# Half of the attention's interleaving copies on ScalarE beside VectorE's, rows of 256 columns in other places and orders, a smaller DMA scratch, six chains moved

## The chip, the cores and the metric

The kernel runs on one core of a Trainium2 chip. Times are device microseconds of one execution, read as the median of several. One execution each is also recorded by the hardware profiler; all views below are of that recorded execution, and its times count from its first instruction. The engines are PE (TensorE: matmuls; PEld is its loading of weights), DVE (VectorE), ACT (ScalarE), POOL (GpSimd) and SP (SyncE, which here only issues DMAs).

## What is computed

Two decoder layers over 256 rows of width 1024, in float32. Cut to what matters:

```python
for i in range(2):
    proj = rms_norm(x, norm_g[i]) @ w_in[i]                  # 1024 x 4096
    rq, rk, rv, rz, mq, mk, mv, mz = split(proj, 8)          # 512 columns = 4 heads of 128 each
    r_out = silu(rz) * group_norm(retention(rotary(rq), rotary(rk), rv)) * ret_norm_g[i]
    m_out = silu(mz) * attention(rms_norm(mq), rms_norm(mk), mv, rel_bias)   # causal, 256 rows
    x = x + concat(r_out, m_out) @ w_out[i]                  # 1024 x 1024
    gate = sigmoid(rms_norm(x) @ w_ple_gate[i])              # 1024 x 1024
    x = x + gate * rms_norm(p[i] @ w_ple[i]) * ple_norm_g[i]
```

With 256 rows there is one block of keys, so the attention is plain causal attention (`moba`), and the retention has two chunks of 128 rows.

## The kernel before, in words

**Precision by three products.** A float32 operand is cut into a high part (rounded to the type fp32r) and a low part (the rest). A product is three matmuls: high by high, high by low, low by high (`mm3`, L386 to L388; `first_rows`, L534, for the first input tiles; `three`, L913, for the scores of attention and retention). The stationary operand is 128x128 of the activations, the moving one a row of 512 weight columns, so most matmuls are 128x512. Three places have rows of 256 columns: the scores (L913: 256 keys, four calls of 12 matmuls), the first four matmuls on the first tile, and the last tile of the last gate projection, which is done in two halves of 256 columns (`gated`, `mm3` with `cols`: 48 matmuls).

**Weights.** Tiles of 128 x 2 x 512 floats (512 KB) are loaded by SP into the ring `wst` (8 buffers), cut on ACT (L336, high part `wh`) and on DVE (L339, low part `wl`) into rings of 5, or into lent space of T, V, PS, K2 and G when the attention doesn't use it. Each weight tile feeds 12 matmuls. The host lays columns of weights in lanes: a row of 512 is read as four runs of 32 pieces of 16 bytes (`columns`, `lanes`).

**Turning activations round.** Results have rows of the sequence on the partitions; the next product needs them the other way. `halves` (L602, ACT) takes a 128x512 float32 tile apart into two planes of 16 bits, `turned` (L607) has SP transpose both planes by one DMA (L612), and two copies on DVE (L621, one for each plane, 128x512 of 16 bits) interleave them again in the target. `to_heads` does that for the queries and keys of both attentions (target T, 8 calls a layer), `probs` for the probabilities (target PS, 3 calls a layer), `to_parts` for the inputs of the next projection (target tmp).

**Order.** All five engines run instructions in the order in which the program is recorded. PE's order is nearly fixed by the code. For the other engines a planner, `Flow`, keeps a clock for each engine, adds an assumed cost for each step and, among the steps that could start, takes the one of the chain with the smallest due time (`key`). `tick` puts the attention's matmul groups between rows of a projection once the chains that they need are done by the planner's clocks. So an assumed cost, a due time or one more buffer moves instructions on ACT, DVE, POOL and SP.

**Around the places that matter.** In layer 0 the order on PE is: first tiles (L534), projections (L386 to L388) with the attention's scores (L931, L913) between them, the attention's sums over values and retention's own scores (L941, L991), retention's scores (L913) and sums (L941), then the output projection. `ret_norm` (L1008 to L1029) and `ret_gate` (L1050 to L1066) follow the retention's sums; the tile that L1057 reads is one of four PSUM banks `acc` that the output projection needs next.

## Time and profile before

| | |
|---|---|
| median of 3 runs | 298.32 us (297.07 to 298.73) |
| the profiled execution | 296.44 us, its span from first to last instruction 294.5 us |
| granted TensorE clock | 1.000 over the span |
| DVE busy | 253.8 us (86%), 461 instructions |
| ACT busy | 214.5 us (73%), 376 instructions |
| POOL busy | 33.1 us (11%) |
| DMA | 69.77 MB, mean 237 GB/s; queue q1 (issued by SP) 78.7% of 16 engines, q0 (issued by POOL) 32 packets |
| last matmul starts | 290.18 us; the tail behind it is one tanh, two VectorE operations and a store |

A matmul's listed duration overlaps the next one, since they are pipelined: what it costs is the distance between starts. An idle time in brackets at the end of a row of the timeline is that of the engine just before it, with what ended it.

### The profile page before, as it was taken

Reading aid. Unit: us, or ns where it says so; the run is one execution under the profiler, and the core shown is the slowest. Engines: PE = TensorE matmul, PEld = TensorE weight load, DVE = VectorE, ACT = ScalarE, POOL = GpSimd, SP = SyncE. Lnnn points to the kernel's source line nnn. Section 1 sums busy time; section 2 is a strip of 40 time slices with the busy share of each in tenths; the row PEclk is TensorE's granted clock in tenths of the full one; section 3 lists DMA queues with packets and bytes.
Section 4 is the critical chain, followed back from the end, with each engine's and each line's share of the span. In section 5 each row is a group of like instructions: output and inputs, shape, how many; then the busy total and the mean of one; then the engine's idle time right before and its main releaser. Section 6 shows DMA issues by size and latency. Waiting matters only on the chain.

```text
span 294.5 us, 4301 instructions
## 1 busy us (share of the span) xinstructions
PE 289.2 (98%) x1411; PEld 247.2 (84%) x1411; DVE 253.8 (86%) x461; ACT 214.5 (73%) x376; POOL 33.1 (11%) x44
## 2 busy tenths in 40 slices
PE   8999999999999999999999999999999999999994
PEld 5888888888899878888888888888898988888894
DVE  4958699979999999699999589999998797969942
ACT  4889965789837893998585896599646869489411
POOL 5005200000001200022003240000000030001200
PEclk9999999999999999999999999999999999999999
DMA  7999989988989958698679969687999776843011
GB/s 233 368 402 416 260 251 330 364 270 164 232 249 248 358 140 280 157 240 329 157 228 258 376 197 254 247 226 168 241 330 238 269 229 181 277 95 71 0 75 71
DMA packets 61774, 69.77 MB, mean 237 GB/s; under 512 B 46260, under 2 KB 47160, under 8 KB 61624
## 3 DMA queue, kind: packets, MB, share of 16 engines
q1 hardware_dynamic: 61712, 69.50, 78.7%
q8 instruction: 11, 0.18, 0.2%
q14 instruction: 11, 0.09, 0.1%
q0 software_dynamic: 32, 0.01, 0.0%
q10 hardware_dynamic: 8, 0.00, 0.0%
HBM read 57.42 MB, written 1.05 MB: 199 GB/s over the span
## 4 chain that ended last, share of the span: by engine, by line
PE 73%; DVE 13%; DMA 5%; ACT 4%; issue 3%; ACTq 0%; DVEq 0%
PE acc L386 20%; PE acc L387 19%; PE acc L388 19%; DVE wl L339 5%; PE acc L534 5%; DMA wst<-in_w_ple 3%; DMA w<-u 2%; PE mix L941 2%; ACT wh L336 2%; DVE T L621 2%; PE mix L282 1%; PE mix L723 1%; PE mix L724 1%; PE mix L725 1%; PE mix L913 1%
## 5 line engine op out<-in xcount | busy, mean ns | idle before, releaser
L386 PE MATMUL acc<-wh,a 128*128 128x512 f32 (+1 forms) x286 | 108.1, 378 | 0.0
L387 PE MATMUL acc<-wl,a 128*128 128x512 f32 (+1 forms) x286 | 107.6, 376 | 0.0
L388 PE MATMUL acc<-wh,a 128*128 128x512 f32 (+1 forms) x286 | 107.5, 376 | 0.0
L339 DVE TENSOR_TENSOR wl<-wst,wh 128x1024 fp32r<-128x1024 f32 x76 | 92.1, 1221 | 7.2 <-ACT wh L336 6.7
L336 ACT CAST wh<-wst 128x1024 fp32r<-128x1024 f32 x76 | 78.5, 1052 | 13.4 <-PE acc L388 4.0
L388 PEld LDWEIGHTS acc<-wh,a 128*128 128x128 f32 x286 | 53.5, 187 | 9.2
L386 PEld LDWEIGHTS acc<-wh,a 128*128 128x128 f32 x286 | 53.5, 187 | 8.9
L387 PEld LDWEIGHTS acc<-wl,a 128*128 128x128 f32 x286 | 53.5, 187 | 8.6
L602 ACT COPY u<-tok 128x1024 uint16<-128x1024 uint16 x30 | 30.9, 1048 | 13.9 <-DVE tok L959 8.9
L638 ACT CAST a<-tmp 128x512 fp32r<-128x512 f32 x20 | 12.4, 618 | 11.0 <-DVE tmp L635 8.3
L654 POOL TENSOR_TENSOR ro<-rs_t,neghalf 128x4 f32<-128x4 f32 x4 | 5.8, 1460 | 127.6 <-DVE rs_t L652 127.6
L602 ACT COPY u<-x_t 128x1024 uint16<-128x1024 uint16 x12 | 12.5, 1042 | 9.8 <-DVE x_t L1119 6.8
L621 DVE COPY tmp<-w 128x512 uint16<-128x512 uint16 x40 | 16.3, 463 | 0.1
L1163 ACT ACTIVATE tmp<-acc,hr 128x512 f32<-128x512 f32 (+1 forms) x9 | 5.7, 638 | 13.4 <-PE acc L388 13.4
L621 DVE COPY T<-w 128x512 uint16<-128x512 uint16 x32 | 12.9, 468 | 2.6 <-DMA w<-u 2.6
L640 DVE TENSOR_TENSOR a<-tmp,a 128x512 fp32r<-128x512 f32 x20 | 13.7, 684 | 0.0
L814 POOL TENSOR_TENSOR qr<-qms,neghalf 128x4 f32<-128x4 f32 x8 | 10.5, 1317 | 11.8 <-DVE qms L812 11.8
L1166 DVE SCALAR_TENSOR_TENSOR tmp<-tmp,E 128x512 f32<-128x512 f32 (+1 forms) x9 | 5.7, 628 | 7.1 <-ACT tmp L1163 7.0
L386 PE MATMUL acc<-T,a 128*128 128x512 f32 (+1 forms) x30 | 11.1, 372 | 0.4 <-DVE tok L1057 0.4
L941 PEld LDWEIGHTS mix<-V,PS 128*128 128x128 f32 x96 | 11.3, 192 | 0.3
L941 PE MATMUL mix<-V,PS 128*128 128x128 f32 x96 | 11.4, 275 | 0.0
L534 PE MATMUL acc<-wh,a 128*128 128x512 f32 (+1 forms) x42 | 11.2, 387 | 0.0
(143 smaller groups left out, 460.9 us busy)
## 6 DMA issues: line engine op xcount, KB each, us to landing
wst<-in_w_in SPq DMA_DIRECT2D x59, 512.0 KB, 6.5
wst<-in_w_out SPq DMA_DIRECT2D x16, 512.0 KB, 7.2
wst<-in_w_gate SPq DMA_DIRECT2D x16, 512.0 KB, 4.6
wst<-in_w_ple SPq DMA_DIRECT2D x4, 512.0 KB, 7.3
wst<-in_early SPq DMA_DIRECT2D x4, 384.0 KB, 6.7
a<-in_early SPq DMA_DIRECT2D x3, 384.0 KB, 5.2
x_t<-in_x SPq DMA_DIRECT2D x1, 1024.0 KB, 11.5
gb<-in_ple_g SPq DMA_DIRECT2D x2, 512.0 KB, 7.0
```

The costliest lines, as they stand in the source:

```text
L336: nc.scalar.copy(hi, s)
L339: nc.vector.tensor_tensor(lo, s, hi.bitcast(F32), op=ALU.subtract)
L386: nc.tensor.matmul(ps, ah, wh, start=start, stop=False)
L387: nc.tensor.matmul(ps, ah, wl, start=False, stop=False)
L388: nc.tensor.matmul(ps, al, wh, start=False, stop=stop)
L534: nc.tensor.matmul(ps[m][:, sl], (a0.lo if which[0] == "lo" else a0.hi)[:, k, m * P:(m + 1) * P], columns(w, sl), start=start and i + j == ...
L602: nc.scalar.copy(u, src.bitcast(U16).rearrange("p (n t) -> p t n", t=2))
L621: nc.vector.tensor_copy(v, w[:, t].rearrange("p (h b) k -> p h (b k)", h=v.shape[1]))
L638: nc.scalar.copy(h, src)
L640: nc.vector.tensor_tensor(a.lo[:, k0:k0 + 4, m * P:(m + 1) * P], src, h.bitcast(F32), op=ALU.subtract)
L814: nc.gpsimd.tensor_tensor(r, t, neghalf[:, :H], op=ALU.pow)
L941: nc.tensor.matmul(ps[:, h * DH:(h + 1) * DH], lhs(h, m, b), v[:, b, h * DH:(h + 1) * DH], start=b == 0, stop=b == m)
```

## The change

Six edits.

1. `turned` takes `beside`. Where it is set (`BESIDE`: for `to_heads` and `probs`, not for `to_parts`), the copy of the second plane is a chain of its own, `other`, on ACT, and runs next to DVE's copy of the first plane; what follows waits for both. That is 22 of the 84 copies.
2. Rows of 256 columns: the tile Q2 (stationary operand of L913) moves from the pool `big` to the pool `cs`, and two gap tiles of 48 floats surround that place, so that it starts 64 bytes past a multiple of 128 bytes in each partition, where it started at a multiple before; K2 (moving) still starts at a multiple. The last gate weights are laid in lanes over groups of 256 columns, and `line_half` reads a half as four runs of 16 pieces, where `columns` read two runs of 32. The 512-wide row of that tile comes out in another column order, which its tanh puts right by its access pattern.
3. `dynamic_dma_scratch_size=4096`, where the default takes 16384 bytes of each partition, and one more buffer of `wst` (9).
4. `LIFT` adds numbers to the due times of six named chains; so the second query tile's norm comes earlier, and a weight load, the copies of two planes, the statistics of the second half of x and a load of layer 1 come later.
5. In `first_rows` the second tile's three products run in the order of the first tile's (low activations before low weights), and its low activations are made before its low weights.
6. The planner's assumed cost of a row of 256 columns: 0.342 for three where it was 0.36, and 0.5 of a row of 512 where it was 0.53.

```diff
-S_BUFS, H_BUFS = 8, 5
+S_BUFS, H_BUFS = 9, 5
+LIFT = {("qk_norm", 1): -5.0, ("gen", 3): 2.0, ("other", 5): 1.0, ("other", 4): 4.0, ("gen", 61): 4.0,
+        ("x_stats", 1): 4.0}
+BESIDE = True, True, False
...
+    def due(self):
+        return (self.key() if callable(self.key) else self.key) + LIFT.get(self.name, 0.0)
...
-    cs.tile([P, 32], F32, name="gap")
+    cs.tile([P, 48], F32, name="gap")
+    ct.tile([P, 48], F32, name="gap")
...
+    def line_half(w, c0):
+        return bass.AP(tensor=w.tensor, offset=w.offset + c0 + (LANES - 1) * LINE,
+                       ap=[w.ap[0], [-LINE, LANES], [LANES * LINE, S // LANES // LINE], [1, LINE]])
...
-        wh, wl = columns(wh, cols), columns(wl, cols)
+        wh, wl = (lanes(w) if cols.stop - cols.start == GW else line_half(w, cols.start) for w in (wh, wl))
...
-        firsts[k, "a"] = flow.begin(first_input(k, src, g), k - (19.6 if k else 19.9), flow.end)
+        firsts[k, "a"] = flow.begin(first_input(k, src, g), k - (19.6 if k > 1 else 19.9), flow.end)
...
-        order = [(("hi", "hi"), wh, None)] + (rows if k == 0 or key else rows[::-1])
+        order = [(("hi", "hi"), wh, None)] + (rows if k < 2 or key else rows[::-1])
...
-    def turned(u, raw, take=()):
+    def turned(u, raw, take=(), beside=False):
...
+        def other():
+            yield ask(ACT, 0.53)
+            copy(nc.scalar.copy, 1)
+            flow.free("w16")
+        if beside:
+            c = flow.begin(other(), Chain.running.key, flow.end - 0.35)
+            copy(nc.vector.tensor_copy, 0)
+            return (c,)
+        copy(nc.vector.tensor_copy, 0)
+        yield ask(DVE, 0.35)
+        copy(nc.vector.tensor_copy, 1)
...
-                both = big.tile([P, 2, H, P], F32R, name="Q2", bufs=1)
-                hi, lo = Q2[name] = both[:, 0], both[:, 1]
+                pair = cs.tile([P, 2, H, P], F32R, name="Q2")
+                hi, lo = Q2[name] = pair[:, 0], pair[:, 1]
...
-            nc.scalar.activation(th, ps, AF.Tanh, scale=HR[m, "v"])
+            if last and n and width == GW:
+                nc.scalar.activation(th.rearrange("p (s t n) -> p s t n", s=2, t=LANES),
+                                     ps.rearrange("p (t s n) -> p s t n", s=2, t=LANES), AF.Tanh, scale=HR[m, "v"])
+            else:
+                nc.scalar.activation(th, ps, AF.Tanh, scale=HR[m, "v"])
...
+    w_gate[DEPTH - 1, 1] = rows(a["w_ple_gate"][DEPTH - 1:], GW, 2, P // LINE // 2)[0, 1]
...
-    nc = bacc.Bacc("TRN2", target_bir_lowering=False, num_devices=1)
+    nc = bacc.Bacc("TRN2", target_bir_lowering=False, num_devices=1, dynamic_dma_scratch_size=4096)
```

PE keeps its instructions and, but for the second first tile and the attention's scores of layer 1 (two rows earlier among the projections), their order.

What moves on the others is shown at three places. Rows are engine order; line numbers are those of the kernel that the rows are from, so L336, L602, L612, L621, L849 before are L353, L624, L634, L642, L886 after.

ACT in layer 0, from the last key tiles of retention to the gap before the attention's sums come back (u is a plane pair on its way to a transpose, w one that came back, V the values, ph an input of the embedding). Before:

```order
L781 CAST K_841<-T 128x4x128
L602 COPY u_863<-tok 128x1024
L602 COPY u_872<-tok 128x1024
L336 CAST wh<-wst 128x1024
L789 CAST Q_890<-T 128x512
L849 ACTIVATE V<-acc,rstd 128x512
L336 CAST wh<-wst 128x1024
L849 ACTIVATE V<-acc,rstd 128x512
L746 CAST ph<-pf 128x512
L336 CAST wh<-wst 128x1024 x3
```

After:

```order
L781 CAST ph<-pf 128x512
L353 CAST wh<-wst 128x1024
L642 COPY PS<-w_840 128x2x256
L642 COPY PS<-w_851 128x2x256
L624 COPY u_897<-tok 128x1024
L353 CAST wh<-wst 128x1024
L886 ACTIVATE V<-acc,rstd 128x512 x2
L353 CAST wh<-wst 128x1024
L642 COPY T<-w_903 128x4x128
L824 CAST Q_945<-T 128x512
L642 COPY T<-w_919 128x4x128
L353 CAST wh<-wst 128x1024 x2
```

Four plane copies stand in this piece now, and the last of them, T from w_919, is retention's second key tile, which L991 on PE reads.

DVE in layer 0, from the rotary steps to the first tile of probabilities (L898, L902 before are L935, L939 after; L839 is L876; L339 is L356). Before:

```order
L833 TENSOR_TENSOR tmp<-acc,cst 128x512
L835 TENSOR_TENSOR tok<-acc,cst 128x512
L339 TENSOR_TENSOR wl<-wst,wh 128x1024 x2
L839 TENSOR_TENSOR tok<-tok,tmp 128x512 x3
L898 TENSOR_TENSOR tok<-mix,tb 128x512
L902 TENSOR_REDUCE nm<-tok 128x4
```

After:

```order
L876 TENSOR_TENSOR tok<-tok,tmp 128x512
L356 TENSOR_TENSOR wl<-wst,wh 128x1024
L870 TENSOR_TENSOR tmp<-acc,cst 128x512
L872 TENSOR_TENSOR tok<-acc,cst 128x512
L935 TENSOR_TENSOR tok<-mix,tb 128x512
L939 TENSOR_REDUCE nm<-tok 128x4
L356 TENSOR_TENSOR wl<-wst,wh 128x1024
L876 TENSOR_TENSOR tok<-tok,tmp 128x512 x2
```

The probabilities stand ahead of two of the three L839 and, counted from the program's start, behind 15 low parts of weights (L339) where they stood behind 16, and behind four plane copies where they stood behind eight.

SP in layer 0, from the last transposes of the queries and keys to the loads behind the gated outputs' transposes (in_w_out, in_w_ple and in_w_gate are weight loads of 512 KB; w_1009 and w_1037 before, w_1020 and w_1045 after, are the attention's outputs; w_1242 after is retention's first). Before:

```order
L612 DMA_TRANSPOSE w_918<-u_872 128x8x128
L326 DMA wst<-in_w_out 128x1024
L302 DMA gb<-in_ple_g 128x1024
L326 DMA wst<-in_w_out 128x1024 x2
L612 DMA_TRANSPOSE w_1009<-u_998 128x8x128
L612 DMA_TRANSPOSE w_1037<-u_1021 128x8x128
L326 DMA wst<-in_w_out 128x1024 x5
L326 DMA wst<-in_w_ple 128x1024 x2
L326 DMA wst<-in_w_gate 128x1024
L612 DMA_TRANSPOSE w_1234<-u_1223 128x8x128
```

After:

```order
L343 DMA wst<-in_w_out 128x1024
L634 DMA_TRANSPOSE w_903<-u_738 128x8x128
L634 DMA_TRANSPOSE w_919<-u_897 128x8x128
L319 DMA gb<-in_ple_g 128x1024
L343 DMA wst<-in_w_out 128x1024 x4
L634 DMA_TRANSPOSE w_1020<-u_1006 128x8x128
L634 DMA_TRANSPOSE w_1045<-u_1029 128x8x128
L343 DMA wst<-in_w_out 128x1024 x3
L343 DMA wst<-in_w_ple 128x1024 x2
L343 DMA wst<-in_w_gate 128x1024 x3
L634 DMA_TRANSPOSE w_1242<-u_1231 128x8x128
```

Five loads of in_w_out stand ahead of the attention outputs' transposes where three stood, and three of in_w_gate ahead of retention's first where one stood.

More of the change, by code (lines that the diff above doesn't have):

```diff
@@ L1 @@
+import collections
 import math
@@ L125, in can @@
         r = max(r, self.dma - self.backlog())
-        if mb and callable(c.key) and r < c.key():
+        if mb and callable(c.key) and r < c.due():
             for o in self.live:
@@ L151, in pick @@
         start, eng, cs = best
-        return start, min((c for r, c in cs if r <= start), key=lambda c: c.key() if callable(c.key) else c.key)
+        return start, min((c for r, c in cs if r <= start), key=Chain.due)
     def lay(self, start, c):
@@ L613, in turned, with copy @@
                           transpose=True)
-        dst = None
-        for t in range(2):
-            yield ask(DVE, 0.35, take=() if t else take)
-            if not t:
-                flow.free("u16")
-                dst = raw()
-            v = dst[:, t]
-            nc.vector.tensor_copy(v, w[:, t].rearrange("p (h b) k -> p h (b k)", h=v.shape[1]))
+        yield ask(DVE, 0.35, take=take)
+        flow.free("u16")
+        dst = raw()
+        def copy(engine, t):
+            v = dst[:, t]
+            engine(v, w[:, t].rearrange("p (h b) k -> p h (b k)", h=v.shape[1]))
+        def other():
[9 more added lines that the diff above has]
+        copy(nc.vector.tensor_copy, 1)
         flow.free("w16")
+        return ()
     def to_parts(a, m, k0, u, g=None):
@@ L630, in raw @@
             return box[0].bitcast(U16).rearrange("p (j k t) -> p t j k", j=4, t=2)
-        yield from turned(u, raw, ("tmp",))
+        both = yield from turned(u, raw, ("tmp",), BESIDE[2])
         src = box[0].rearrange("p (k t) -> p k t", k=4)
         if g is not None:
-            yield ask(DVE, 0.605)
+            yield ask(DVE, 0.605, after=both)
             nc.vector.tensor_tensor(src, src, g[:, :, None].to_broadcast([P, 4, P]), op=ALU.mult)
-        yield ask(ACT, 0.53)
+        yield ask(ACT, 0.53, after=both)
         h = a.hi[:, k0:k0 + 4, m * P:(m + 1) * P]
@@ L768, in raw @@
                 return T[name].bitcast(U16).rearrange("p h (k t) -> p t h k", t=2)[:, :, :, m * P:(m + 1) * P]
-            yield from turned(u, raw, () if m else ("T",))
+            both = yield from turned(u, raw, () if m else ("T",), BESIDE[0])
             t = slice(m * P, (m + 1) * P)
@@ L773, in to_heads @@
             if name == MQ and not m:
-                yield ask(ACT, 0.64)
+                yield ask(ACT, 0.64, after=both)
                 nc.scalar.activation(src, src, AF.Copy, scale=scale)
             elif name in (MK, RQ):
-                yield ask(ACT, 0.53, take=() if m else ("K2",))
+                yield ask(ACT, 0.53, take=() if m else ("K2",), after=both)
                 if not m:
@@ L784, in to_heads @@
             elif (name, m) in ((MQ, 1), (RK, 0)):
-                yield ask(ACT, 0.64, take=("Q2",))
-                both = big.tile([P, 2, H, P], F32R, name="Q2", bufs=1)
-                hi, lo = Q2[name] = both[:, 0], both[:, 1]
+                yield ask(ACT, 0.64, take=("Q2",), after=both)
+                pair = cs.tile([P, 2, H, P], F32R, name="Q2")
+                hi, lo = Q2[name] = pair[:, 0], pair[:, 1]
                 if scale is None:
@@ L796, in to_heads @@
                     nc.vector.scalar_tensor_tensor(lo, src, scale, hi.bitcast(F32), op0=ALU.mult, op1=ALU.subtract)
+            elif both:
+                yield ask(DVE, 0.0, after=both)
         def qk_norm(g, m, ps):
@@ L908, in probs @@
             raw = box["PT"].bitcast(U16).rearrange("p h (k t) -> p t h k", t=2)
-            yield from turned(u, lambda: raw[:, :, h0:h0 + per, m * P:m * P + n])
+            both = yield from turned(u, lambda: raw[:, :, h0:h0 + per, m * P:m * P + n], beside=BESIDE[1])
+            if both:
+                yield ask(DVE, 0.0, after=both)
         def three(ps, w, x):
@@ L1238, with laned, rows @@
     consts = _constants()
-    def laned(w):
-        return w.reshape(*w.shape[:-1], -1, LANES, P // LINE, LINE)[..., ::-1, :, :].swapaxes(-3, -2).reshape(w.shape)
-    def rows(w, n, half):
+    def laned(w, runs=P // LINE):
+        return w.reshape(*w.shape[:-1], -1, LANES, runs, LINE)[..., ::-1, :, :].swapaxes(-3, -2).reshape(w.shape)
+    def rows(w, n, half, runs=P // LINE):
         L, K, N = w.shape
-        t = laned(w).reshape(L, half, K // P // half, P, N // n, n)
+        t = laned(w, runs).reshape(L, half, K // P // half, P, N // n, n)
         return np.ascontiguousarray(t.transpose(0, 4, 1, 3, 2, 5))
```

15 lines of the change are left out of this document (11 added, 4 removed).

## The prediction

> **What bounds the kernel now.** I read the page's busy times first, then what PE waited for.
>
> ```profile
> PE 289.2 (98%) x1411; PEld 247.2 (84%) x1411; DVE 253.8 (86%) x461; ACT 214.5 (73%) x376; POOL 33.1 (11%) x44
> PE acc L386 <- DVE tok L1057: 0.4, 1, 0.4
> ```
>
> PE is busy for 98% of the span, and apart from its start the list of its waits has one entry, the row shown. So nearly all of the span of 294.5 us is PE's own stream of matmuls, and DVE, ACT and the loads matter only where they make PE late. An edit can gain in two ways: PE's rows get shorter, or a place where PE stands still closes. I looked for both in the timeline. Rows of 512 columns and the one large hole:
>
> ```profile
> 105.07 0.38 PE L387 MATMUL acc<-T,a 128*128 128x512 f32 x1
> 105.29 0.39 PE L388 MATMUL acc<-T,a 128*128 128x512 f32 x1
> 106.13 0.50 PE L386 MATMUL acc<-T,a 128*128 128x512 f32 x1 [0.45 <-DVE tok L1057]
> 106.47 0.39 PE L387 MATMUL acc<-T,a 128*128 128x512 f32 x1
> ```
>
> Starts lie 0.22 apart. At 106.13 the distance is 0.84, at 106.47 it is 0.34: 0.62 and 0.12 lost, **0.74 us** together. A smaller hole is at the start, where pairs follow each other:
>
> ```profile
> 7.54 0.62 PE L534 MATMUL acc<-wh,a 128*128 128x512 f32 x2
> 8.00 0.72 PE L534 MATMUL acc<-wl,a 128*128 128x512 f32 x2
> 8.56 0.60 PE L534 MATMUL acc<-wh,a 128*128 128x512 f32 x2
> ...
> 7.22 0.72 DVE L499 TENSOR_TENSOR wl<-a,wh 128x512 fp32r<-128x512 f32 x1 [0.30 <-ACT wh L440]
> 7.87 0.47 DVE L504 SCALAR_TENSOR_TENSOR a<-a 128x256 fp32r<-128x256 f32 x1
> ```
>
> A pair takes 0.46, the pair at 8.00 takes 0.56, since the low weights are ready only at 7.94: 0.10 lost.
>
> **The change, part by part.**
>
> *Rows of 256 columns.* Four calls of 12 at L913 and 48 in the last gate tile:
>
> ```profile
> 83.56 1.59 PE L913 MATMUL mix<-K,Q 128*128 128x256 f32 x12
> 85.00 0.39 PE L386 MATMUL acc<-wh,a 128*128 128x512 f32 x1
> ...
> 285.10 0.28 PE L387 MATMUL acc<-wl,a 128*128 128x256 f32 x1
> 285.22 0.28 PE L388 MATMUL acc<-wh,a 128*128 128x256 f32 x1
> ...
> L913 PE MATMUL mix<-K,Q 128*128 128x256 f32 x48 | 6.5, 286 | 0.0
> L388 PE MATMUL acc<-wh,a 128*128 128x256 f32 x12 | 3.4, 282 | 0.0
> L388 PE MATMUL acc<-T,a 128*128 128x256 f32 x4 | 1.1, 282 | 0.0
> ```
>
> (L386 and L387 have as many, so 3 x 16 = 48.) Twelve in 85.00 - 83.56 = 1.44 make 0.120 each; the gate's are 0.12 apart too. Half a row of 512 would be 0.110. The trace has no row in the new places or orders, so the bounds are 96 x 0.010 = 0.96 us gained and, as a place can also be a worse one, as much a row lost at L913, 0.48. The gate's halves get the four-run pattern of the 512-wide rows, so I take those rows for them, 48 x 0.010 = 0.48. At L913 only the weights' address moves by 64 bytes; the nearest row is its own, and I take a quarter, 0.12. Together **0.6 us**, all on PE's stream.
>
> [...]
>
> *The hole at 8.00.* The low activations (0.47 long) now come before the low weights on DVE, and PE takes them in that order. DVE's L448 for this tile ends at 6.92, so they are ready at about 7.4, and the low weights, pushed back by 0.1 to 8.05, are wanted only at 8.44. **0.10 us** goes; the next tile's blocks have been loaded, so nothing is late behind it.
>
> *The copies.* Prices: what DVE loses and ACT gains.
>
> ```profile
> L602 ACT COPY u<-tok 128x1024 uint16<-128x1024 uint16 x30 | 30.9, 1048 | 13.9 <-DVE tok L959 8.9 <-DVE tok L839 3.8 <-DVE tok L817 0.5
> L781 ACT CAST K<-T 128x512 fp32r<-128x512 f32 x8 | 4.9, 625 | 2.8 <-DVE T L621 2.8
> L621 DVE COPY T<-w 128x512 uint16<-128x512 uint16 x32 | 12.9, 468 | 2.6 <-DMA w<-u 2.6
> ```
>
> 32 copies take 12.9 us of DVE, 0.40 each; 22 leave, 8.8 us. ACT has no such copy in the trace: it is bounded by the 512-wide cast, 0.625, and the 1024-wide copy, 1.048; same number of elements, so 0.625, 22 x 0.625 = 13.8 us more on ACT, 11 copies or 6.9 us a layer. In itself this is worth nothing, as PE waits for none of these copies. It pays through the hole at 106.13. Its chain, and the next place behind it:
>
> ```profile
> 102.32 1.05 ACT L602 COPY u<-tok 128x1024 uint16<-128x1024 uint16 x1
> 103.86 1.50 ACT L1029 ACTIVATE T<-mix,mr,ro 128x128 f32<-128x128 f32 x4
> 105.39 0.69 DVE L1057 TENSOR_TENSOR tok<-T,acc 128x512 f32<-128x512 f32 x1 [0.48 <-ACT T L1029]
> 110.45 0.68 DVE L640 TENSOR_TENSOR a<-tmp,a 128x512 fp32r<-128x512 f32 x1
> 111.18 0.19 PEld L388 LDWEIGHTS acc<-K,a 128*128 128x128 f32 x1
> ```
>
> L602 starts when DVE has finished the first retention tile, the four L1029 follow a tanh on ACT, L1057 follows them, and PE's bank is free at its end, 106.08. DVE itself is late here, and it has hardly been idle; the columns are PE, PEld, DVE, ACT and POOL busy, clock, DMA share and GB/s:
>
> ```profile
> 56.00:84.00 28.00, 28.00 (x146) 24.38 (x145) 26.08 (x45) 23.16 (x41) 0.00 (x0) 1.00 0.95 237
> ...
> 80.30 0.79 DVE L621 COPY T<-w 128x512 uint16<-128x512 uint16 x2
> 81.33 1.06 PE L991 MATMUL mix<-T 128*128 128x128 f32 x8
> ...
> 97.39 1.05 ACT L336 CAST wh<-wst 128x1024 fp32r<-128x1024 f32 x1 [0.98 <-DMA wst<-in_w_out]
> ```
>
> In that stretch seven copies (2.8 us) leave DVE, so it reaches the attention's outputs up to 2.8 us sooner. What may be late next is ACT's cast at 97.39, which waited 0.98 for a load of in_w_out; five of these loads are now issued ahead of the outputs' transposes where three were, and the ninth buffer lets them. 0.74 of lead is enough, and I count most of the hole as closed, **0.6 us**; the bounds are 0 and 0.74.
>
> *The rest.* The smaller scratch frees the bytes of the ninth buffer, and only the bias's DMA of 32 packets comes from POOL; cost nothing, since L898 wants it at 54.69 first. The due times move x's load (1 MB) ahead of the fourth weight tile's (512 KB):
>
> ```profile
> 10.00:20.00 10.00, 10.00 (x47) 8.48 (x46) 8.41 (x14) 8.23 (x19) 0.00 (x0) 1.00 1.01 379
> ...
> 18.24 0.38 PE L386 MATMUL acc<-wh,a 128*128 128x512 f32 x1
> ...
> 21.11 1.09 ACT L336 CAST wh<-wst 128x1024 fp32r<-128x1024 f32 x1
> ```
>
> That tile was cut at 21.11, and PE, at 12 rows of 0.22 a tile from 18.24, takes it at 26.2; 2.8 us later (1.05 MB at 379 GB/s) leaves 2.3, which just covers ACT's 1.09 and DVE's cut of 1.2: cost nothing, though without that cover each us late is a us lost. The planner's assumed costs do no work of their own.
>
> **Sum:** 0.6 + 0.1 + 0.6 = 1.3 us off the span, 293.2. The profiled execution had 296.44, 1.9 outside its span, and would have 295.1. The median of the runs, 298.32, lies 1.9 above it; I take the same 1.3 off it: **297.0 us**.
>
> **The rivals.**
>
> *The wait moves.* In the rows above, L640 ends at 111.13, and PEld takes its tile at 111.18, at once: whatever PE gains at 106 it stands still for at 111, unless that chain leads as well. It goes through a transpose which now has three gate loads ahead of it where it had one. Two more of 512 KB, 1.3 to 2 us, could eat the lead. Then only rows and start are left, 0.7: 297.6.
>
> *The rows stay at 0.12*, the edit not doing what it says: hole and start are left, 0.7: 297.6. [...]
>
> *Deeper loads.* The timed runs took 0.6 to 2.3 us more than the profiled one. If that is loads coming late, the ninth buffer takes another 1 us off: 296.0. No row shows it.
>
> *ACT becomes the bound* (the slower side). The place is L991: PE wants retention's second key tile at 81.33 and had it at 80.30 + 0.79 = 81.09. Seven ACT copies, 4.4 us, stand between 60 and that tile, in a stretch where ACT has 28.0 - 23.2 = 4.8 us idle, most of it behind it:
>
> ```profile
> 77.25 2.96 ACT L336 CAST wh<-wst 128x1024 fp32r<-128x1024 f32 x3
> 83.82 1.05 ACT L602 COPY u<-tok 128x1024 uint16<-128x1024 uint16 x1 [3.60 <-DVE tok L959]
> ```
>
> ACT was through at 80.2; two of the three casts are now behind the tile, so it would come at 80.2 - 2.0 + 4.4 = 82.6, 1.5 us late, and in layer 1 the same: 3.0 lost, 0.7 gained, 300.6. It decides once ACT starts this stretch less than 1.5 us sooner than before. Against it speaks DVE's order ahead of it:
>
> ```profile
> 47.28 1.05 PE L931 MATMUL mix<-T 128*128 128x128 f32 x8
> ...
> 50.61 2.35 DVE L339 TENSOR_TENSOR wl<-wst,wh 128x1024 fp32r<-128x1024 f32 x2
> 52.88 1.90 DVE L839 TENSOR_TENSOR tok<-tok,tmp 128x512 f32<-128x512 f32 x3
> 54.69 0.69 DVE L898 TENSOR_TENSOR tok<-mix,tb 128x512 f32<-128x512 f32 x1
> ...
> 53.60 1.99 ACT L602 COPY u<-tok 128x1024 uint16<-128x1024 uint16 x2 [3.06 <-DVE tok L839]
> ```
>
> The first probabilities (L898) now pass two L839 (1.27), one L339 (1.18) and four copies (1.6): 4.0 us sooner, with PE's scores there since 48.3. ACT's exponentials then fall into the 3.06 it sat idle.
>
> **How the numbers follow.** Forecast 0.42; the wait moves 0.20; rows unchanged 0.10; deeper loads 0.14; ACT the bound 0.14. A measurement of this kernel can tell about 0.5%, 1.5 us, from no change, so the line is at 296.8: the forecast lies 0.2 inside it, and with the bounds of its terms (0.96 and 0.74, so up to 1.8) near half of it, 0.20, is past the line; with all of the deeper loads, faster 0.34. ACT as the bound gives slower in most of its cases, 0.11. The rest, 0.55, is within. The range reaches from 295.6 (deeper loads with the terms at their bounds) to 299.2 (ACT late in one layer).
>
> **What would show it.** Starts of L913 and of the last gate's rows 0.110 to 0.115 apart (rows right), 0.12 (wrong). No bracket at L386 near 105 and none at 111 (the lead held); a bracket at L388 near 110 to 111 with DVE L640 (the wait moved). L991 with idle time behind ACT's copy into T (ACT is the bound). No hole in the pairs at 8. I am wrong altogether if PE waits for weights (L336, L339) or for transposes somewhere that had none.

## The result, and the profile after

| | before | after |
|---|---|---|
| median (7 runs each) | 297.25 us (296.88 to 298.73) | 300.41 us (299.39 to 301.81) |
| ratio of after to before | | 1.0101, 95% interval 1.0072 to 1.0131 |
| profiled execution, its span | 296.44 us, 294.5 us | 301.73 us, 299.8 us |
| PE busy, DVE busy, ACT busy | 289.2, 253.8, 214.5 us | 290.8, 247.0, 227.4 us |

The change made the kernel 3.2 us slower; 297.0 was forecast, 299.2 was the top of the range. The 297.0 is 1.3 off 298.32, a median of three runs; beside seven runs before has 297.25, so the forecast gain of 1.3 would come to 296.0, and the miss is about 4.5 us. The profiled execution of before was among its shortest, that of after among its longest, so the two spans differ by 5.3 us and not by 3.2.

The page of the kernel after: busy times, and the groups of DVE's cuts of weights and of the new copies on ACT (count, busy us, mean ns, idle before and what ended it):

```profile
PE 290.8 (97%) x1411; PEld 246.8 (82%) x1411; DVE 247.0 (82%) x439; ACT 227.4 (76%) x398; POOL 32.7 (11%) x44
L356 DVE TENSOR_TENSOR wl<-wst,wh 128x1024 fp32r<-128x1024 f32 x76 | 91.9, 1217 | 13.0 <-ACT wh L353 12.3
L642 ACT COPY T<-w 128x512 uint16<-128x512 uint16 x16 | 12.6, 803 | 1.1 <-DMA w<-u 1.1
```

The list of PE's waits, where before had one entry apart from the start (us in total, times, longest):

```profile
PE acc L408 <- DVE tok L1096: 1.5, 1, 1.5
PE mix L980 <- ACT V L886: 1.0, 1, 1.0
PE mix L298 <- PEq L1322: 0.8, 1, 0.8
PE mix L952 <- DVE tok L998: 0.6, 1, 0.6
PE acc L556 <- ACT wh L501: 0.4, 1, 0.4
PE acc L410 <- DVE her L744: 0.3, 1, 0.3
PE mix L1030 <- ACT T L642: 0.2, 1, 0.2
```

(L408 to L410 were L386 to L388, L1096 was L1057, L980 was L941, L952 was L913, L1030 was L991.) The entry that was to go, L1096, has grown; five are new. The hole itself, in the timeline of after:

```profile
104.99 1.05 ACT L624 COPY u<-tok 128x1024 uint16<-128x1024 uint16 x1
106.53 1.50 ACT L1068 ACTIVATE T<-mix,mr,ro 128x128 f32<-128x128 f32 x4
106.93 0.38 PE L410 MATMUL acc<-T,a 128*128 128x512 f32 x1
108.06 0.69 DVE L1096 TENSOR_TENSOR tok<-T,acc 128x512 f32<-128x512 f32 x1 [0.48 <-ACT T L1068]
108.80 0.49 PE L408 MATMUL acc<-T,a 128*128 128x512 f32 x1 [1.49 <-DVE tok L1096]
```

The same chain as before (L602, L1029, L1057 in the prediction's rows), but each link 2.7 us later: 104.99 for 102.32, 106.53 for 103.86, 108.06 for 105.39. PE itself is only 1.6 us later (106.93 for 105.29), so it stands still for the 0.73 of before and 1.03 more, about 1.75 us.

To see where PE lost time I added up, from the start times of its matmuls, what each stands further from the one ahead than the usual 0.221, 0.120 or 0.112 us for 512, 256 and 128 columns (only where over 0.015). One execution of each kernel; the labels are those of the experiments below:

| us lost in the stretch | 0 to 10 | 62 to 100 | 100 to 112 | 112 to 200 | 200 to end | sum |
|---|---|---|---|---|---|---|
| before | 0.68 | 0.18 | 0.73 | 0.08 | 0.18 | 1.9 |
| after | 1.09 | 1.53 | 1.75 | 0.82 | 2.33 | 7.6 |
| e3, rows only | 1.12 | 0.22 | 0.78 | 0.35 | 0.18 | 2.7 |
| e11, order of after, copies on VectorE | 0.51 | 1.26 | 0.93 | 0.84 | 0.18 | 3.8 |
| e13, after with three buffers | 0.74 | 2.67 | 0.93 | 0.89 | 0.18 | 5.5 |
| e2, after with packed copies | 0.74 | 1.87 | 1.45 | 0.87 | 0.18 | 5.2 |
| e14, copies on GpSimd | 1.12 | 0.18 | 0.00 | 1.21 | 0.18 | 2.8 |
| e9, order of e3, copies on ScalarE | 0.76 | 3.68 | 0.94 | 0.29 | 1.62 | 7.4 |
| e4, rows and copies on ScalarE | 0.75 | 2.41 | 0.91 | 0.79 | 2.21 | 7.2 |
| e10, order of e4, copies on VectorE | 1.14 | 0.18 | 0.00 | 0.56 | 0.18 | 2.1 |

After minus before is 5.7 us; 0.4 of it is the start, 1.35 the stretch to the retention of layer 0, 1.0 the hole at 106, 2.15 layer 1. (10 to 62 is 0.08 or 0.09 in each.) Not all of it is the copies': e11 has after's order without copies on ScalarE, and after minus e11 is 0.6 at the start, 0.3 from 62 to 100, 0.8 at the hole and 2.15 in layer 1. Most of the 1.35 comes with the order. One execution each is a rough measure: those of after and e11 took 1.3 us more than the medians of their runs, that of before 0.8 less.

### The profile page after: what moved, and what is told of

Read it like the earlier page. It is cut to its first block, busy times and chain, and to the rows that moved or that the text cites. A ratio compares the mean times of both kernels' runs of the same rounds, so it can differ in the third digit from the quotient of the medians.

```text
span 299.8 us, 4284 instructions
## 1 busy us (share of the span) xinstructions
PE 290.8 (97%) x1411; PEld 246.8 (82%) x1411; DVE 247.0 (82%) x439; ACT 227.4 (76%) x398; POOL 32.7 (11%) x44
## 3 DMA queue, kind: packets, MB, share of 16 engines
HBM read 57.42 MB, written 1.05 MB: 195 GB/s over the span
## 5 line engine op out<-in xcount | busy, mean ns | idle before, releaser
L408 PE MATMUL acc<-wh,a 128*128 128x512 f32 (+1 forms) x286 | 107.9, 377 | 0.0
L410 PE MATMUL acc<-wh,a 128*128 128x512 f32 (+1 forms) x286 | 107.6, 376 | 0.0
L356 DVE TENSOR_TENSOR wl<-wst,wh 128x1024 fp32r<-128x1024 f32 x76 | 91.9, 1217 | 13.0 <-ACT wh L353 12.3
L353 ACT CAST wh<-wst 128x1024 fp32r<-128x1024 f32 x76 | 78.8, 1053 | 4.5 <-DMA wst<-in_w_in 2.2
L410 PEld LDWEIGHTS acc<-wh,a 128*128 128x128 f32 x286 | 53.5, 187 | 9.0
L408 PEld LDWEIGHTS acc<-wh,a 128*128 128x128 f32 x286 | 53.5, 187 | 8.9
L624 ACT COPY u<-tok 128x1024 uint16<-128x1024 uint16 x30 | 31.4, 1053 | 8.4 <-DVE tok L998 7.2
L624 ACT COPY u<-x_t 128x1024 uint16<-128x1024 uint16 x12 | 12.5, 1042 | 11.5 <-DVE x_t L1158 7.8
L673 ACT CAST a<-tmp 128x512 fp32r<-128x512 f32 x20 | 12.4, 618 | 10.7 <-DVE tmp L670 7.2
L642 DVE COPY tmp<-w 128x512 uint16<-128x512 uint16 x40 | 16.1, 460 | 2.5 <-DMA w<-u 2.3
L980 PE MATMUL mix<-V,PS 128*128 128x128 f32 x96 | 12.2, 280 | 1.3 <-ACT V L886 1.0
L980 PEld LDWEIGHTS mix<-V,PS 128*128 128x128 f32 x96 | 11.4, 191 | 2.5 <-ACT V L886 2.3
L642 ACT COPY T<-w 128x512 uint16<-128x512 uint16 x16 | 12.6, 803 | 1.1 <-DMA w<-u 1.1
L942 ACT ACTIVATE tok<-tok,nm 128x128 f32<-128x128 f32 (+1 forms) x16 | 7.1, 446 | 7.8 <-DVE nm L939 7.8
L408 PE MATMUL acc<-T,a 128*128 128x512 f32 (+1 forms) x30 | 11.1, 370 | 1.5 <-DVE tok L1096 1.5
L556 PE MATMUL acc<-wh,a 128*128 128x512 f32 (+1 forms) x42 | 11.1, 384 | 0.4 <-ACT wh L501 0.4
L851 POOL TENSOR_TENSOR qr<-qms,neghalf 128x4 f32<-128x4 f32 x8 | 10.0, 1258 | 12.3 <-DVE qms L849 9.3
L1206 ACT ACTIVATE tmp<-acc,hr 128x512 f32<-128x512 f32 (+1 forms) x8 | 5.1, 632 | 8.2 <-PE acc L410 8.2
```

The source lines that it names most:

```text
L353: nc.scalar.copy(hi, s)
L356: nc.vector.tensor_tensor(lo, s, hi.bitcast(F32), op=ALU.subtract)
L408: nc.tensor.matmul(ps, ah, wh, start=start, stop=False)
L410: nc.tensor.matmul(ps, al, wh, start=False, stop=stop)
L556: nc.tensor.matmul(ps[m][:, sl], (a0.lo if which[0] == "lo" else a0.hi)[:, k, m * P:(m + 1) * P], columns(w, sl), start=start and i + j == ...
L624: nc.scalar.copy(u, src.bitcast(U16).rearrange("p (n t) -> p t n", t=2))
```

## The experiments

Ratios are against runs of the kernel before on the same chip, beside the experiment's. They are not quotients of the medians; a difference in us is a difference of ratios, of 297.5 us, unless two times stand beside it.

| run | what it is | median us | ratio (95% interval) |
|---|---|---|---|
| e1 | after, copies back on VectorE, planned anew | 299.90 | 1.0082 (1.0055 to 1.0109) |
| e2 | after, order kept, copies packed | 298.59 | 1.0045 (1.0026 to 1.0065) |
| e3 | before + rows of 256 and the smaller scratch | 296.93 | 0.9980 (0.9967 to 0.9993) |
| e4 | e3 + copies on ScalarE, planned anew | 300.81 | 1.0120 (1.0103 to 1.0137) |
| e5 | e3 + nine buffers | 298.07 | 1.0013 (0.9993 to 1.0034) |
| e6 | e3 + start's order | 299.54 | 1.0065 (1.0045 to 1.0085) |
| e7 | e3 + four due times | 298.91 | 1.0051 (1.0026 to 1.0075) |
| e8 | e4, planner told 0.70 us a copy | 302.68 | 1.0167 (1.0136 to 1.0198) |
| e9 | order of e3, copies on ScalarE | 301.50 | 1.0152 (1.0115 to 1.0188) |
| e10 | order of e4, copies on VectorE | 297.97 | 1.0019 (0.9998 to 1.0039) |
| e11 | order of after, copies on VectorE | 296.61 | 0.9984 (0.9964 to 1.0005) |
| e12 | e3, planner told 0.36 for 0.35 | 297.88 | 1.0001 (0.9978 to 1.0024) |
| e13 | after, order kept, three transposed buffers | 299.22 | 1.0043 (1.0021 to 1.0065) |
| e14 | order of after, copies on GpSimd | 297.42 | 0.9994 (0.9976 to 1.0013) |
| e15 | order of after, 6 copies (probabilities) on ScalarE | 298.14 | 1.0020 (1.0007 to 1.0033) |
| e16 | order of after, 16 copies (queries, keys) on ScalarE | 299.04 | 1.0034 (1.0010 to 1.0057) |
| e17 | order of e3, copies on GpSimd | 297.45 | 1.0000 (0.9984 to 1.0017) |
| e18 | e3, planner told 0.34 for 0.35 | 297.70 | 1.0011 (0.9995 to 1.0027) |

**Taking parts out, each with a new plan.**

```diff
 # e1, from after
-BESIDE = True, True, False
+BESIDE = False, False, False
 # e3, from e1: eight buffers, LIFT empty, the start as before
-S_BUFS, H_BUFS = 9, 5
+S_BUFS, H_BUFS = 8, 5
-LIFT = {("qk_norm", 1): -5.0, ("gen", 3): 2.0, ("other", 5): 1.0, ...
+LIFT = {}
-k - (19.6 if k > 1 else 19.9)
+k - (19.6 if k else 19.9)
-(rows if k < 2 or key else rows[::-1])
+(rows if k == 0 or key else rows[::-1])
 # e4, from e3
-BESIDE = False, False, False
+BESIDE = True, True, False
```

> The changed kernel with all 44 interleaving copies of the attention on VectorE again; rows of 256, the ninth buffer, the start's order and the smaller scratch stay, and so do the due times of the chains that still exist (two of the six belonged to ScalarE's copies). Theory (ScalarE, with 22 copies of 0.80 us, comes late between 62 and 80 us and in the same stretch of layer 1): the stops of PE at 81.5, 84.9, 106.9 and 222 to 238 go or fall back to before's 0.74 us at 106, PE's lost time falls from 7.6 to about 2 us, and the time is 296.3 to 297.0 us, 0.6 under before by the rows. Rival (the ninth buffer, the loads' new order or the due times cost it): it stays at about 300 us with the copies gone.

> The kernel before with the rows of 256 alone (their places and orders, and the smaller scratch that makes the room): copies on VectorE, eight buffers, old start, old due times. Theory: rows of 256 start 0.114 apart, 96 times 0.006 is 0.6 us less, the hole of 0.74 at 106 and the one of 0.10 at 8 us stay, time 296.5 to 296.9, ratio 0.997 to 0.999. Rival (the rows' new places cost elsewhere, or the scratch does): 297.3 or more.

> The same kernel (rows of 256, eight buffers, old start, old due times) with the 22 copies on ScalarE: it differs from the run of the rows alone by the copies only. Theory (the copies cost it, whatever the due times): ScalarE late before the retention of both layers, 2 to 4 us of stops there, time 299 to 301. Rival (the six moved chains or the ninth buffer spoil it): no more than 0.7 us over the rows alone, about 297.

e3 and e4 came out as the theory had them: the rows gain 0.2%, and the copies on top of them cost 1.4%, 4.2 us. In the traces of before and e3 every engine runs the same instructions in the same order, so e3's gain is not that of another plan. But e1 spoke for the rival: with the copies back on VectorE most of the loss is still there, 299.90. So I put the other parts on e3 one at a time: nine buffers (e5), the start's order (e6), the four due times (e7).

> The kernel of the rows alone (copies on VectorE, old start, old due times, 296.93 us) with nine weight buffers in place of eight. Putting the copies back left the changed kernel at 299.9, so one of buffer, start and due times costs some 3 us by itself. Theory (the ninth buffer lets weight loads go ahead of the transposes and of what else shares the queue): 299 or more, with stops of PE at weights or transposes that the rows alone don't have. Rival (a due time or the start does it): within 0.7 us of 296.9.

> The kernel of the rows alone with the changed order of the start (low activations ahead of low weights at the second tile, its due time 0.3 earlier). My step: the hole of 0.10 at 8 us goes, 296.8. Rival (the start's order alters the planner's later choices, or its blocks now wait on a late load): 298 or more.

> The kernel of the rows alone with the four changed due times that exist without ScalarE's copies: x's load ahead of the fourth weight tile, a normalisation of layer 0 earlier by 5, a load of layer 1 and a statistic of layer 0 later by 4. Theory (the due times were fitted to ScalarE's copies and are wrong without them): 298 to 300, with a stop at 18 us if the load of x is the cause and at 111 if the normalisation or the statistic is. Rival (the due times are harmless, the ninth buffer costs): within 0.7 of 296.9.

Each costs something: 1.0, 2.5 and 2.1 us by the ratios. None shows a mechanism of its own. e6, whose edit touches the first 10 us, loses its time far behind them (its waits of PE; apart from L298 at the start they stand at 138 and 84 us):

```profile
PE acc L410 <- DVE her L744: 1.2, 1, 1.2
PE mix L298 <- PEq L1322: 0.8, 1, 0.8
PE mix L952 <- DVE tok L998: 0.6, 1, 0.6
```

Nothing that runs there is changed; the planner has put the same instructions in another order. Hence two kernels in which only a number of the planner differs:

```diff
 # e12 (0.36) and e18 (0.34), from e3, at both copies
-yield ask(DVE, 0.35 ...
+yield ask(DVE, 0.36 ...
```

> The kernel of the rows alone with a number of the planner changed and nothing else: VectorE's interleaving copy is planned at 0.36 us in place of 0.35. No instruction is added, removed or changed; some change places. Theory B (any new order loses to the one that the kernel had, whatever the reason for it): 298 to 300. Rival (a new order is worth nothing by itself; the nine buffers, the start and the due times each cost by what they do): within 0.7 us of 296.9.

> The kernel of the rows alone with VectorE's copy planned at 0.34 in place of 0.35 and nothing else: the second draw of what an order is worth by itself (0.36 gave 297.88, 0.95 over the rows alone). If orders scatter by about 1 us: anywhere from 296.5 to 298.5. If most of the places stay as they are here (14 rows of PE's list differ, where 0.36 had 231), within 0.5 us of 296.9.

They are 0.6 and 0.9 us above e3, with no work changed; e18's interval lies just clear of e3's, e12's overlaps it. e12's new stop is a wait of the retention's sums, `PE mix L980 <- DVE PS L1019`, 1.2 us, where e3 has none. Over the nine orders with all copies on VectorE (e1, e3, e5, e6, e7, e10, e11, e12, e18; some with the ninth buffer, the start's order or the due times too) the ratio runs from 0.9980 to 1.0082, 3 us. So an edit that is planned anew is measured with an unknown of that size, and e1 and e4 prove little about the copies.

**Order held.** The second copy of a pair is issued on another engine, while the planner still plans as before, so PE, POOL and SP keep every row. In e9 it stays at its place in the program; in e10 and e11 VectorE makes it right behind the first.

```diff
 # e9, from e3 (the flag is set, but only chooses the engine)
-        copy(nc.vector.tensor_copy, 1)
+        copy(nc.scalar.copy if beside else nc.vector.tensor_copy, 1)
 # e10, from e4, and e11, from after
         def other():
             yield ask(ACT, 0.53)
-            copy(nc.scalar.copy, 1)
...
-            copy(nc.vector.tensor_copy, 0)
+            copy(nc.vector.tensor_copy, 0); copy(nc.vector.tensor_copy, 1)
```

> The order that was planned for copies on VectorE (the rows alone, 296.93 us), but the second of each pair of the attention's copies is issued on ScalarE at the same place of the program; PE, POOL and SP keep every row. It separates where the copies run from the order that the planner makes of it. Theory A (ScalarE has no room for 22 copies of 0.80 us): 299 to 301, with VectorE's weight cuts idle behind ScalarE's casts and stops of PE near 81, 106 and 235 us. Theory B (the new order is the loss, the copies' engine is not): within 0.7 us of 296.9.

> The order that was planned for copies on ScalarE (rows and copies, 300.81 us), but VectorE makes both copies, one behind the other, where it made the first; ScalarE makes none. Theory A (ScalarE's 17.6 us are the loss): 297 to 298.5. Theory B (the order is the loss): 300 to 301.5, with the stops at 68, 85, 107, 137 and 236 us still there.

> The changed kernel (300.41 us) in its own order, with both copies of each pair on VectorE. Theory A (ScalarE's time): 297 to 298.5, the stops at 84.9, 106.9 and 237 us gone. Theory B (the order): 299.7 or more. The packed copies, 0.17 us shorter on each engine, took 1.8 us off in this same order, so between: about 298.5 if half of the loss is ScalarE's time.

| | copies on VectorE | copies on ScalarE | difference |
|---|---|---|---|
| order of e3 | 0.9980 | 1.0152 | 1.7%, 5.1 us |
| order of e4 | 1.0019 | 1.0120 | 1.0%, 3.0 us |
| order of after | 0.9984 | 1.0101 | 1.2%, 3.5 us |

In all three orders the engine decides, and in the order of after the copies are the whole loss: with them on VectorE the ratio is e3's, within 0.2% either way. VectorE's idle time behind ScalarE's casts, which the next section follows, grows with the copies in each order: 7.0 to 15.4 us, 7.2 to 11.6, 6.5 to 12.3. A plan that is told a longer copy doesn't help either, 302.68 us for e4's 300.81:

```diff
 # e8, from e4
-            yield ask(ACT, 0.53)
+            yield ask(ACT, 0.70)
```

> The kernel of rows and copies (eight buffers, old start and due times, 300.81 us) with the planner told 0.70 us from copy to copy on ScalarE in place of 0.53 (copies last 0.80 and overlap by 0.1). Theory (ScalarE has no room for 17.6 us more there, whatever the plan): 299.5 or more. Rival (the plan was wrong because of the price): 298 or less.

**How ScalarE's time reaches PE.** In the page of e11, against that of after, with PE's order the same, the cuts' idle time halves:

```profile
L356 DVE TENSOR_TENSOR wl<-wst,wh 128x1024 fp32r<-128x1024 f32 x76 | 91.5, 1215 | 6.6 <-ACT wh L353 6.5
```

The timelines show how. ACT and DVE of after, 67 to 84 us:

```profile
67.63 1.43 ACT L642 COPY T<-w 128x512 uint16<-128x512 uint16 x2
68.92 1.04 ACT L624 COPY u<-tok 128x1024 uint16<-128x1024 uint16 x1
69.85 1.04 ACT L353 CAST wh<-wst 128x1024 fp32r<-128x1024 f32 x1
70.93 1.23 DVE L356 TENSOR_TENSOR wl<-wst,wh 128x1024 fp32r<-128x1024 f32 x1 [1.36 <-ACT wh L353]
...
79.79 0.78 ACT L642 COPY T<-w 128x512 uint16<-128x512 uint16 x1 [0.15 <-DMA w<-u]
80.60 0.62 ACT L824 CAST Q<-T 128x512 fp32r<-128x512 f32 x1
81.12 0.76 ACT L642 COPY T<-w 128x512 uint16<-128x512 uint16 x1
81.75 1.98 ACT L353 CAST wh<-wst 128x1024 fp32r<-128x1024 f32 x2
82.82 1.23 DVE L356 TENSOR_TENSOR wl<-wst,wh 128x1024 fp32r<-128x1024 f32 x1 [0.53 <-ACT wh L353]
83.96 0.17 DVE L989 RECIPROCAL ri<-den 128x4 f32<-128x4 f32 x1
```

and of e11, the same places:

```profile
80.73 0.80 DVE L642 COPY T<-w 128x512 uint16<-128x512 uint16 x2
82.00 1.22 DVE L356 TENSOR_TENSOR wl<-wst,wh 128x1024 fp32r<-128x1024 f32 x1
83.13 0.18 DVE L989 RECIPROCAL ri<-den 128x4 f32<-128x4 f32 x1
```

Two copies, a copy for the transposes and then the cast stand in a row on ACT; DVE's next instruction is the cut of that cast's tile, and it waits 1.36 us. At 82.82 the same again, and behind that cut stands L989, the first step of the attention's outputs, now at 83.96: 0.83 later than in e11, and 1.85 later than before (82.11); the other 1.0 came with the order. From there up to 106 DVE's chain is 1.85 to 2.7 us behind that of before, and the hole inherits it. The windows show ACT's room going (PE, PEld, DVE, ACT busy; first before, then after, then e11):

```profile
80.00:84.00 4.00, 4.00 (x32) 3.79 (x31) 3.85 (x11) 0.40 (x2) 0.00 (x0) 1.00 0.97 313
200.00:225.00 25.00, 25.00 (x137) 21.97 (x136) 23.77 (x43) 17.30 (x21) 0.00 (x0) 1.00 0.89 246
...
80.00:84.00 4.00, 3.85 (x29) 3.52 (x29) 3.47 (x6) 3.70 (x5) 0.00 (x0) 1.00 0.75 241
200.00:225.00 25.00, 24.86 (x123) 21.17 (x122) 21.50 (x30) 24.41 (x36) 0.00 (x0) 1.00 0.88 215
...
80.00:84.00 4.00, 3.95 (x30) 3.57 (x29) 3.85 (x9) 2.26 (x3) 0.00 (x0) 1.00 0.98 301
200.00:225.00 25.00, 25.00 (x131) 21.79 (x130) 24.54 (x43) 19.09 (x23) 0.00 (x0) 1.00 0.90 250
```

In layer 1 ACT is busy 24.4 us of 25, where it was 17.3 before and 19.1 in e11. The other way would be the two buffers of transposed tiles, which the slower engine of a pair sets free:

```diff
 # e13, from after
-        w = tok_p.tile([P, 2, 4, P], U16, name="w16", bufs=W_BUFS)
+        w = tok_p.tile([P, 2, 4, P], U16, name="w16", bufs=3)
```

> The changed kernel, every instruction in its place, with three buffers for transposed tiles where there were two (the planner still counts two). Theory W (ScalarE's late copy keeps a transposed buffer, and so SP's next transpose and all loads queued behind it, waiting): the transposes near 75 to 77 us issue some 1 us sooner and the time falls to 299.5 or less. Theory C (ScalarE's casts are late behind the copies, and VectorE's weight cuts wait for them in order): time within 0.5 us of 300.4, VectorE's idle time behind ScalarE's casts still about 12 us.

SP's transposes of after and of e13, the next one issued (us it spends on the queue's engine, count):

```profile
75.08 3.50 SPq L634 DMA_TRANSPOSE w<-u  x2
...
73.60 5.43 SPq L634 DMA_TRANSPOSE w<-u  x2
```

It is issued 1.5 us sooner, and the time is 0.6% less than after's, 1.7 us: theory W's time, and not C's. But the table of lost time says that the gain isn't where these transposes are. Layer 1's 2.15 us are gone, layer 0 is not better (2.67 and 0.93 for 1.53 and 1.75), and DVE still waits 14.1 us for ACT's casts in all, which was C's sign. So by these profiles the buffers matter in layer 1, and the casts are left in layer 0. The wait in layer 1, in after: the retention's values V on ACT stand behind L673, whose transposed input, the attention's outputs, comes late.

```profile
237.03 0.62 ACT L673 CAST a<-tmp 128x512 fp32r<-128x512 f32 x1 [0.27 <-DVE tmp L642]
237.56 0.68 ACT L886 ACTIVATE V<-acc,rstd 128x512 f32<-128x512 f32 x1
238.29 0.86 PEld L980 LDWEIGHTS mix<-V,PS 128*128 128x128 f32 x7 [1.22 <-ACT V L886]
```

The time to landing of the four transposes from 215 to 232 us, in after and in e13:

```profile
DMA to landing us min/median/max: 3.0/3.1/4.7
...
DMA to landing us min/median/max: 3.0/3.1/3.3
```

The first transpose of the outputs is issued at 229.07 in after and at 228.41 in e13, and is the one that takes 4.7 us in after and 3.1 in e13: 2.25 us later in all, of which the buffers' queue explains 0.66. Why it lands slower in after no run shows. In e11 it is issued at 224.17, 4.9 us ahead of after, with PE only 2.1 us ahead (L952 at 225.53 for 227.61). There the outputs' two transposes take 3.9 and 4.4 us to land, and PE doesn't stop: without ScalarE's copies there is room for such a delay.

**The price of a copy.** To make ACT's copy shorter with every instruction in its place:

```diff
 # e2, from after
-            v = dst[:, t]
-            engine(v, w[:, t].rearrange("p (h b) k -> p h (b k)", h=v.shape[1]))
+            v = dst[:, t] if not beside else packed(dst, t)
+            engine(v, w[:, 1 if beside else t].rearrange("p (h b) k -> p h (b k)", h=v.shape[1]))
```

> The changed kernel with every instruction in the same order; only the copies that ScalarE shares with VectorE write packed runs instead of every second element, both from the high halves. It leaves the interleaving of the shared copies out. If the write to every second element is what makes ScalarE's copy 0.80 us, it takes 0.62 here (as its cast of 512), ScalarE reaches 80 us some 1.4 us sooner (8 copies of 0.18), the stop at 81.5 (0.4 us) goes, the one at 106.9 (1.75) falls below 0.7, layer 1's 2.1 falls by half or more, and the time is 298 to 298.7. If two-byte elements are the cost, the copy stays at 0.80 and the time at 300.4. Rival (the order of the instructions, not the price of the copy, is the loss): the copy is shorter and the time stays within 0.5 us of 300.4.

The groups of e2 by shape:

```profile
L642 ACT COPY T<-w 128x512 uint16<-128x512 uint16 x16 | 9.9, 634 | 0.9 <-DMA w<-u 0.8
L642 DVE COPY T<-w 128x512 uint16<-128x512 uint16 x16 | 4.6, 290 | 4.4 <-DMA w<-u 4.2
```

Packed, the copy takes 0.63 on ACT in place of 0.80, and 0.29 on DVE in place of 0.47; the time falls by 0.6%, 1.7 us, as expected, and by the two profiles nearly all of it in layer 1. The stop at 81 that was to go did not, and that at 106 fell by 0.3 only. So of the 3.5 us about half hangs on the price (on both engines; the run doesn't part them), and at 0.63, the price that the prediction had, the copies still cost 1.0045 over 0.9984, 1.8 us. In time on ACT the price matters less than it looks, since instructions there overlap: copies in a row start 0.64 us apart in after and 0.52 in e2, and ACT is busy 227.4 us in after, 225.0 in e2 and 213.9 in e11.

**Which copies.**

```diff
 # e15 (e16 with != and == changed over), from after; BESIDE = 1, 2, 0
-            copy(nc.scalar.copy, 1)
+            copy(nc.scalar.copy, 1) if beside == 2 else None
...
-            copy(nc.vector.tensor_copy, 0)
+            copy(nc.vector.tensor_copy, 0); copy(nc.vector.tensor_copy, 1) if beside != 2 else None
```

> The changed kernel's order with only the 6 copies of the probabilities on ScalarE; the 16 of queries and keys are on VectorE. Against 296.61 with none on ScalarE and 300.41 with 22. If the loss goes by the number: 297.6. If the copies of queries and keys are what holds the stretch ahead of the retention: within 0.7 us of 296.6.

> The changed kernel's order with only the 16 copies of queries and keys on ScalarE, those of the probabilities on VectorE. By the number: 299.4. If the copies of queries and keys carry the loss: 300 or more, with the stops at 84.9, 106.9 and 237 us.

Over e11 the 6 cost 0.36% (1.1 us) and the 16 cost 0.5% (1.5 us), together 2.6 of 3.5. So no one kind carries the loss. By the number they would cost 0.95 and 2.5; the 16 fall short of that by 1 us, about as much as the intervals leave open. The profiles of both lack layer 1's stops, which stand only where both kinds are on ScalarE.

**An engine with room.** e14 is e11, e17 is e9, with `nc.gpsimd.tensor_copy` for the second copy.

> The changed kernel's order with the second copy of each pair on GpSimd, which is busy for 11%. If the loss is ScalarE's time, VectorE and ScalarE are both relieved: 296 to 297 where GpSimd's copy takes about 1 us. If GpSimd's copy takes 1.5 us or more, or holds VectorE up, the attention's chain is late by that and the time is 298 to 301. No run has shown the price of such a copy on GpSimd.

> The order of the rows alone (296.93 us) with the second copy of each pair on GpSimd, at the same place of the program; the run with ScalarE in its place took 301.5. If ScalarE's time was the loss there, this one has none of its stops: 296 to 297, and the hole of 0.78 at 106 closes as it did with GpSimd in the changed kernel's order, for VectorE has 8 us less to do; 296.2 then. If the move itself (the longer way through a second engine, about 1.1 us a copy) is a loss, 297.5 or more.

GpSimd in ScalarE's place takes 1.1 and 1.5% off, so the loss is ScalarE's time and not the way through a second engine. Yet nothing is won over VectorE alone. In e14 the hole at 106 is closed (0.00 in the table), in e17, where it was to close as well, 0.74 of it is left and the time is 297.45 for the expected 296.2. Nor does the hole depend on the copies alone: with all of them on VectorE it is 0.00 in e6, e7 and e10, of which the first two are slower than before. Groups of e14:

```profile
L642 POOL COPY T<-w 128x512 uint16<-128x512 uint16 x16 | 16.9, 1068 | 40.4 <-DMA w<-u 36.0
L642 DVE COPY T<-w 128x512 uint16<-128x512 uint16 x16 | 8.6, 539 | 1.2 <-DMA w<-u 0.9
L356 DVE TENSOR_TENSOR wl<-wst,wh 128x1024 fp32r<-128x1024 f32 x76 | 95.0, 1261 | 4.5 <-ACT wh L353 4.3
```

VectorE has 22 copies fewer than in e11 and is busy longer, 255.5 us for 254.1: its cuts take 1.261 for 1.215 us (3.5 us over 76), its own copies into T 0.54 for 0.46. In e17 the cuts take 1.224 for e3's 1.216, the copies into T 0.59 and those into PS 0.86 for 0.46, and VectorE is busy 253.1 us for 253.7.

## Why the prediction was wrong, step by step

**The rows: right, the size a third too large.** They stand 0.113 to 0.115 apart on the mean. The last gate tile of after, and a call of L952 in e3:

```profile
290.14 0.27 PE L408 MATMUL acc<-wh,a 128*128 128x256 f32 x1
290.25 0.27 PE L409 MATMUL acc<-wl,a 128*128 128x256 f32 x1
290.37 0.28 PE L410 MATMUL acc<-wh,a 128*128 128x256 f32 x1
...
83.94 1.54 PE L952 MATMUL mix<-K,Q 128*128 128x256 f32 x12
85.32 0.39 PE L408 MATMUL acc<-wh,a 128*128 128x512 f32 x1
```

1.38 for twelve where it was 1.44. From the start times, the gate's 48 rows took 5.33 us for 5.55 and the four calls of L952 in e3 5.72 for 5.89: 0.40 us, for 0.48 + 0.12 forecast. The gate's part was too large (0.22), since the four-run pattern did not reach 0.110; L952's quarter was about right (0.18). The whole of e3 is 0.6 us (0.2 to 1.0) under before. The rival that the rows stay at 0.12 is out. Why the new places and orders are quicker no run shows.

**The hole at 8: right, and not to be seen in the time.** In after the pairs stand 0.45 and 0.44 apart:

```profile
7.54 0.61 PE L556 MATMUL acc<-wl,a 128*128 128x512 f32 x2
7.99 1.04 PE L556 MATMUL acc<-wh,a 128*128 128x512 f32 x4
8.87 0.38 PE L556 MATMUL acc<-wl,a 128*128 128x512 f32 x1
```

In that execution a load of in_early came 0.8 us later than before's and PE lost 0.4 more over the first 10 us. Over the eighteen experiments these 10 us lost 0.5 to 1.7, which buries 0.1.

**The copies: this is the step that failed.** "In itself this is worth nothing, as PE waits for none of these copies. It pays through the hole at 106.13." That was to gain 0.6 us; with the order held, the copies cost 3.5 us (5.1 and 3.0 in the two other orders). What was put at nothing is the waiting behind them. PE waits for hardly a copy (0.2 us, at L1030), but ACT's weight casts stand behind the copies, DVE's cuts wait for the casts in order, and the attention's chain stands behind the cuts; DVE's wait for casts is 6.5 us in e11 and 12.3 in after. Queues behind the moved instruction were named for SP's loads and not for this. So the attention's outputs, which DVE was to reach "up to 2.8 us sooner", came 0.83 us later than in the same order without ScalarE's copies, 1.85 later than before; and the hole that was to close grew by 0.8 against e11, by 1.0 against before. The transposed buffers, now held until the later engine is done, were not priced at all; a third one gives back 1.7 us.

The price was too low as well, by less than it looks. 0.625 came from a cast that writes packed words; the copy writes every second element and takes 0.80, 17.6 us by its rows and not 13.8. As neighbours overlap, ACT's busy time rose by 13.5 us over e11, close to the 13.8, and DVE's fell by 7.1 for the 8.8 forecast. With packed copies (e2) it rose by 11.1, and 1.8 us are still lost. So the room was about right in sum; what it would hold up was not.

**The rival that came true had the engine, not the way.** "ACT becomes the bound" gave 300.6 at a chance of 0.14; 300.41 was measured. That the two are so near is partly luck: the rival's loss was 2.3 us on a start of 298.32, the measured one is 3.2 on 297.25. The sign that it named is there, L1030 (L991 before) waiting for ACT's copy into T, but that place lost 0.42 us in layer 0, not 1.5, and layer 1 lost at V's product. (In e3's order, e9, the same place lost 1.6 us.) What spoke against it held: the first exponentials started at 53.01 for 56.45, 3.4 us sooner. But those 3.4 us were used up before 80, and the rival should have been priced by ACT's room over the whole stretch (4.8 us of 28) against the 4.4 us that were put into it. That alone said that any delay would have nothing to run into; in after ACT is busy 26.2 us of that stretch.

**"The rest" at nothing.** x's load ahead of the fourth tile: no stop between 10 and 62 us in after, as forecast. The ninth buffer, the start and the due times: in after's order they cost nothing together (e11 against e3, 0.04%, with 0.2% either way). By themselves they cost 1.0 to 2.5 us; for the start that comes through the order that the planner then makes, as e6's stops far behind it show, for the other two this is likely and not shown. "The planner's assumed costs do no work of their own" is true and was the wrong thing to conclude from: 0.01 us in one number moved the time by 0.6 to 0.9 us, half of the forecast gain or more. The stop near 138 us (0.58 in after) is of this kind: e11 and e14 have it with no copy on ScalarE, e3 doesn't.

**The other rivals.** The wait did not move to 111; PE lost nothing there. Deeper loads gave nothing that shows.

**A version that beats both.** e3, the rows alone, is the only one whose whole interval lies under before: 296.93 us, 0.998. e11 is as fast (296.61), its interval touches 1. e12 and e18 have e3's rows in other orders, and neither is faster than before.

Open: why layer 1's stops need both kinds of copies, and why the transpose there lands slower; how DVE's wait for the casts divides between layers and stops, which no run takes out by itself; how much of e2's gain is ScalarE's part; and whether a plan exists in which ScalarE's copies pay, since only four orders were tried.

## What to carry to other kernels

Before work is moved to an engine that is "only 73% busy", look at the stretch it lands in and at what stands behind it in that engine's queue, and follow from there which other engine waits in order; an engine that PE never waits for can hold up the one it does. Price an instruction by a row with the same element size and write pattern, or give it a range up to the next costlier row (here 0.625 to 1.05, and it was 0.80). Where a planner sets the order, test an edit with the order held: taking it out and planning anew measured the order (e1 is 2.9 us above e11, where the same copies are on VectorE) and not the edit.
